# Norm factors spread by TensorE transposes, and gated y stored in two parts: a two-layer decoder trunk on one core

## The chip, the cores and the metric

The kernel runs on one NeuronCore of a Trainium2 chip. The metric is the time of one execution on the device in microseconds; lower is better. All times below are microseconds unless marked otherwise. TensorE is called PE in the profile (its weight loads PEld), VectorE DVE, ScalarE ACT, GpSimd POOL and SyncE, whose queue issues the DMAs, SP.

## The reference

The input is one sequence of 1024 positions with 1024 features. Layer 0 mixes by a gated linear recurrence (LRU), layer 1 by attention with a forget gate (FoX) in 16 heads of 64. Both have a SiLU gate path, and an RMS norm stands before each layer and at the end.

```
def rms_norm(x, g):
    y = xf * lax.rsqrt(jnp.mean(xf * xf, axis=-1, keepdims=True) + EPS)
    return y * g

for i in range(2):
    h = rms_norm(x, norm_g[i])
    x = x + (lru_mixer(h, ...) if i == 0 else fox_mixer(h, ...))
return rms_norm(x, final_g)

# fox_mixer
u = h @ w_in;  q, k, v, gate, f_logit = parts of u
cum = cumsum(log_sigmoid(f_logit + b_f))
logits = q @ k.T * scale + cum[query] - cum[key], causal
o = softmax(logits) @ v
return (o * silu(gate)) @ w_out
```

## The kernel before

Activations lie features by positions: a tile has 128 features on its partitions and 512 positions, a half of the sequence, along the free dimension. To keep float32 accuracy with the faster `float32r` products, each operand is split in a high part (a cast) and a low part (operand minus high part), and each product is three matmuls: high by high, low weight by high, high weight by low. `to_hi` and `to_lo` make the parts; in the profile a cast on ACT is at line 87 and a subtraction at line 98.

The norm needs 1/rms of each position as a row on all partitions. `inv_rms` sums the squares over the features by matmuls with a column of ones (`sscol`), which leaves four columns `rms`, one for each block of 128 positions, with a position on each partition. ACT takes the root and DVE the reciprocal. DVE then multiplies the identity with each column, which gives four diagonal blocks in `rs` (line 153), and one full float32 matmul of a matrix of ones with `rs` sums over the partitions, so that every partition holds the whole row (`rsrow`, line 155). ACT copies it to `rs`. This is done four times, for two halves in each layer.

Layer 1 walks over heads in pairs. For head `hd`, `maxima` makes the scores S of 128 queries against all earlier keys, DVE masks them and takes the maximum, and ACT makes the exponentials p with their sums. `weigh` transposes p on PE (tile `pt`), ACT and DVE split the result in `ph` and `pl`, and PE multiplies both with the values into `O`. Scores and transposed p share two PSUM buffers of two banks each (tag `S`): a new one can be written only when the last reader of the one before the last is through. The sums go through DRAM (`recd`) to come back as a row on 64 partitions (`recb`); POOL multiplies the gate `sg` with it (`scale`, line 765), and after the odd head of a pair the output `yo` with `sg` (`gated`, line 820). For heads 1 to 11 `gated` stores yo to DRAM (`y1d`, line 826), one tile for each of two halves and six pairs.

Beside the attention PE does fill work: the projections of the next pair's keys, queries and gate (`kq_units`, `g_units`, tiles `gps`), and of the next values (`vps`). The gate's projection takes a tanh on ACT into a tile `t` of tag `xp` with two buffers. At heads 12 and 13 the fill is the gate of the last pair and the output projection (`partial`, tile `ops`) of the six stored pairs: `load_y` loads y, `split_loaded` splits it a pair at a time through `beside`, after a named exponential (`seen`) on ACT and a named mask (`masked`) on DVE.

The order on each engine is set by a scheduler at build time from the order of the program text, buffers that come free, and `issue_after`. On the chip each engine then works through its own list in that order.

## Time and profile before

| | |
|---|---|
| median of 3 runs | 1113.87 (1113.86 to 1114.06) |
| the profiled execution's own time | 1113.94 |
| its span, first to last instruction | 1112.2 |
| granted TensorE clock | 1.000 |
| busy: PE, DVE, ACT, POOL | 99%, 68%, 52%, 15% |
| moved by DMA | 105.43 MB |
| 16 products of identity and rms (line 153), DVE | 5.3 |
| 12 casts and 12 subtractions of loaded y, ACT and DVE | 6.8, 9.4 |

The span leaves out what lies before the first and after the last instruction, 1.7 here. Matmuls are pipelined, so their durations overlap: what one costs PE is read from the start of one to the start of the next. In a timeline row a number in brackets is the idle time of that engine just before, with what ended it.

### The profile page before, as it was taken

How to read it: one execution, taken by the hardware profiler on the slowest of the kernel's cores; microseconds unless marked ns; L12 is line 12 of the kernel's file. 1: busy time of each engine (PE TensorE's matmuls, PEld its weight loads, DVE VectorE, ACT ScalarE, POOL GpSimd, SP SyncE). 2: the span in 40 equal slices, each digit the busy share in tenths (PEclk: the TensorE clock that was granted, in tenths of full speed). 3: DMA queues.
4: the chain of work that ended last, by engine and by line, in shares of the span. 5: the costliest groups of instructions: out<-in, count | busy, mean ns of one | idle time of the engine just before them, and what ended most of it. 6: DMA issues, size and time to landing. Idle time of an engine off the chain costs nothing.

```text
span 1112.2 us, 15778 instructions
## 1 busy us (share of the span) xinstructions
PE 1101.9 (99%) x5697; PEld 935.1 (84%) x5697; DVE 755.0 (68%) x1266; ACT 582.4 (52%) x1075; POOL 166.1 (15%) x120
## 2 busy tenths in 40 slices
PE   9999999999999999999999999999999999999997
PEld 7787888888888888988888988889888898878886
DVE  8888755876669687756676566765667655576645
ACT  8487445355453665544555355544555544454435
POOL 1222212111111201421110100101002020010110
PEclk9999999999999999999999999999999999999999
DMA  6111111111112113443334224242142431655444
GB/s 239 48 57 43 51 54 43 48 53 42 62 35 75 48 54 129 129 112 118 101 90 103 91 69 109 72 113 96 53 122 75 103 108 38 185 159 185 142 147 189
DMA packets 63558, 105.43 MB, mean 95 GB/s; under 512 B 9364, under 2 KB 24340, under 8 KB 63480
## 3 DMA queue, kind: packets, MB, share of 16 engines
q1 hardware_dynamic: 63480, 104.42, 31.1%
q8 instruction: 45, 0.74, 0.3%
q14 instruction: 33, 0.27, 0.1%
HBM read 63.30 MB, written 15.93 MB: 71 GB/s over the span
## 4 chain that ended last, share of the span: by engine, by line
PE 93%; issue 3%; DVE 1%; ACT 1%; POOL 1%; DMA 1%; SPq 0%; DVEq 0%; POOLq 0%; ACTq 0%
PE gps L57 33%; PE ops L57 17%; PE ups L57 10%; PE vps L57 8%; PE S L57 6%; PE O L57 6%; PE pt L61 6%; PE turn L57 3%; PE gate L57 2%; POOL wl L98 1%; PE sscol L57 0%; DMA x<-in_xt 0%; DVE hl L232 0%; PE rsrow L57 0%; DMA wf<-in_w 0%
## 5 line engine op out<-in xcount | busy, mean ns | idle before, releaser
L57 PE MATMUL gps<-hh,wh 128*128 128x512 f32 x576 | 228.2, 396 | 0.0
L57 PE MATMUL gps<-hh,wl 128*128 128x512 f32 x576 | 225.6, 392 | 0.2 <-POOL wl L98 0.2
L57 PE MATMUL gps<-hl,wh 128*128 128x512 f32 x576 | 225.5, 392 | 0.0
L87 ACT CAST wh<-wf 128x512 fp32r<-128x512 f32 (+2 forms) x156 | 94.0, 607 | 141.8 <-PE gps L57 56.0
L736 ACT ACTIVATE p<-S,m 128x128 f32<-128x128 f32 (+7 forms) x128 | 94.9, 741 | 140.0 <-DVE m L731 139.1
L98 POOL TENSOR_TENSOR wl<-wf,wh 128x512 fp32r<-128x512 f32 (+1 forms) x60 | 95.6, 1600 | 382.2 <-ACT wh L87 321.7
L98 DVE TENSOR_TENSOR pl<-pt,ph 128x512 fp32r<-128x512 f32 (+1 forms) x198 | 98.7, 540 | 77.0 <-ACT ph L87 76.3
L57 PEld LDWEIGHTS gps<-hl,wh 128*128 128x128 f32 x576 | 108.2, 188 | 23.8
L57 PEld LDWEIGHTS gps<-hh,wl 128*128 128x128 f32 x576 | 108.5, 188 | 19.2 <-POOL wl L98 0.6
L57 PEld LDWEIGHTS gps<-hh,wh 128*128 128x128 f32 x576 | 108.5, 188 | 19.0
L731 DVE CUSTOM_DVE_ANT_0 S<-S,mask 128x128 f32<-128x128 f32 (+7 forms) x128 | 97.3, 760 | 34.2 <-PE S L57 29.6
L765 POOL TENSOR_TENSOR sg<-sg,recb 64x512 f32<-64x512 f32 x32 | 42.8, 1356 | 441.9 <-DMA recb<-recd 407.3
L87 ACT CAST ph<-pt 128x512 fp32r<-128x512 f32 (+1 forms) x198 | 83.5, 472 | 29.1 <-PE pt L61 23.9
L57 PE MATMUL S<-T,U 96*128 96x512 f32 (+7 forms) x384 | 91.7, 347 | 0.0
L98 DVE TENSOR_TENSOR wl<-wf,wh 128x512 fp32r<-128x512 f32 x96 | 68.3, 719 | 24.6 <-ACT wh L87 23.8
L375 DVE TENSOR_TENSOR x<-x,ops 128x512 f32<-128x512 f32 x80 | 54.1, 681 | 40.3 <-PE ops L57 40.3
L57 PEld LDWEIGHTS S<-T,U 128*128 128x128 f32 (+1 forms) x384 | 68.7, 189 | 12.5 <-ACT p L736 0.2
L61 PE MATMUL pt<-ident,p 128*128 128x128 f32 x576 | 79.2, 273 | 0.0
L61 PEld LDWEIGHTS pt<-ident,p 128*128 128x128 f32 x576 | 67.5, 140 | 11.5 <-issue 2.1
L57 PE MATMUL ups<-hh,wh 128*128 128x512 f32 x192 | 75.4, 394 | 1.0 <-ACT hh L89 0.4
L57 PE MATMUL ups<-hh,wl 128*128 128x512 f32 x192 | 75.0, 391 | 0.6 <-POOL wl L98 0.6
L57 PE MATMUL ups<-hl,wh 128*128 128x512 f32 x192 | 75.2, 391 | 0.2 <-DVE hl L232 0.2
(163 smaller groups left out, 2245.4 us busy)
## 6 DMA issues: line engine op xcount, KB each, us to landing
wf<-in_w SPq DMA_DIRECT2D x100, 256.0 KB
wf<-in_wo SPq DMA_DIRECT2D x64, 128.0 KB
U<-qkh SPq DMA_DIRECT2D x64, 128.0 KB
T<-qkh SPq DMA_DIRECT2D x28, 256.0 KB
x1d<-x SPq DMA_DIRECT2D x16, 256.0 KB
wf<-in_wv SPq DMA_DIRECT2D x16, 256.0 KB
U<-qkl SPq DMA_DIRECT2D x32, 128.0 KB
xp<-x1d SPq DMA_DIRECT2D x16, 256.0 KB
```

Source lines behind the costliest of these rows:

```text
L57: pe[0] = nc.tensor.matmul(*args, **kw)
L61: pe[0] = nc.tensor.transpose(*args)
L87: nc.scalar.copy(hi, src)
L98: return eng.tensor_tensor(lo, src, f32(hi), ALU.subtract)
L375: nc.vector.tensor_tensor(x, x, pt, ALU.add)
L731: masked[0] = nc.vector.tensor_tensor_reduce(S[:, :n], S[:, :n], mask[:, SEQ - n :], -1.0, -NEG, ALU.add, ALU.min, accum_out=m)
L736: seen[0] = nc.scalar.activation(p, S[:, :n], AF.Exp, bias=m, scale=-1.0, accum_out=sums[:, i : i + 1])
L765: nc.gpsimd.tensor_tensor(sg, sg, recs[hd // 2][rows, part], ALU.mult)
```

## The change

It has two parts. In `inv_rms` the four products with the identity and the float32 matmul go. Instead PE transposes, for each block of 128 positions, a matrix all of whose 128 columns are the same column of `rms`: the column is read with a step of zero. Each partition of the result holds the row.

In `gated`, for heads 1 to 11, yo is split at once: a cast on ACT to `yh`, a tile of tag `xp`, after the exponential last recorded, and a subtraction on DVE in place, after the mask last recorded. Both parts are stored. `load_y` loads both, and the splits at heads 12 and 13 go, with `split_loaded` and `beside`.

```
-        nc.vector.reciprocal(rms, rms)
+        done = nc.vector.reciprocal(rms, rms)
+        row = ps.tile([P, HALF], F32, tag="O", name="rsrow")[:, : nb * P]
         for b in range(nb):
-            done = nc.vector.tensor_scalar(rs[:, b * P : (b + 1) * P], ident, rms[:, b : b + 1], None, ALU.mult)
-        row = ps.tile([P, HALF], F32, tag="O", name="rsrow")[:, : nb * P]
-        inst = matmul(row, onesf, rs, start=True, stop=True)
+            inst = transpose(row[:, b * P : (b + 1) * P], rms[:, b : b + 1].to_broadcast([P, P]), ident)
         nc.scalar.copy(rs, row)
...
-    y1d = dram.tile([2, KT, P, HALF], F32, name="y1d")
+    y1d = dram.tile([2, KT, 2, P, HALF], F32, name="y1d")
...
             elif hd < 13:
-                nc.sync.dma_start(y1d[c, pair], yo)
+                yh = at.tile([P, HALF], F32R, tag="xp", name="yh", bufs=2)
+                with tc.issue_after(seen[0].ins):
+                    to_hi(yh, yo, nc.scalar)
+                with tc.issue_after(masked[0].ins):
+                    to_lo(yo.bitcast(F32R), yo, yh, nc.vector)
+                for part, y in enumerate((f32(yh), yo)):
+                    nc.sync.dma_start(y1d[c, pair, part], y)
...
             for pair in range(6):
-                nc.sync.dma_start(f32(pair_of_y(c, pair)[1]), y1d[c, pair])
+                for part, y in enumerate(pair_of_y(c, pair)):
+                    nc.sync.dma_start(f32(y), y1d[c, pair, part])
...
-                        beside(g_units(7, (1,)), 0, splits[0]),
+                        g_units(7, (1,)),
                         load_y(1),
-                        beside(beside(partial(todo), 0, splits[0]), 2, splits[1]),
+                        partial(todo),
```

The order of the instructions moves at three kinds of place. First, ACT in head 1, from the exponential of 256 score columns on (p, from S and the maximum m; t is the gate's tanh, wh the high part of a weight, ph of transposed p). Before:

```order
L736 ACTIVATE p,sums<-S,m 128x256
L701 ACTIVATE t_4757<-sg_4630 128x512
L87 CAST ph<-pt 128x512 x2
L736 ACTIVATE p,sums<-S,m 128x384
L87 CAST wh<-wf 128x512
L87 CAST ph<-pt 128x512
L87 CAST ph<-pt 128x384
L736 ACTIVATE p,sums<-S,m 128x512
```

And of the changed kernel, the same stretch:

```order
L735 ACTIVATE p,sums<-S,m 128x256
L87 CAST ph<-pt 128x512 x2
L735 ACTIVATE p,sums<-S,m 128x384
L87 CAST yh<-yo 128x512
L700 ACTIVATE t_4757<-sg_4626 128x512
L87 CAST wh<-wf 128x512
L87 CAST ph<-pt 128x512
L87 CAST ph<-pt 128x384
L735 ACTIVATE p,sums<-S,m 128x512
```

The cast of yo stands behind the exponential of 384 columns, and the tanh, which stood ahead of it, now stands behind the cast; heads 5 and 9 have the same order. Second, DVE in the changed kernel at the same place, from the mask of 384 columns on (S to S with its maximum; `ISA m` reads the maximum out; wl and pl are low parts):

```order
L730 ISA S,m<-S,mask 128x384
L730 ISA m 128x1
L98 TENSOR_TENSOR yo<-yo,yh 128x512
L701 SCALAR_TENSOR_TENSOR sg_4626<-t_4757,sg_4626 128x512
L98 TENSOR_TENSOR wl<-wf,wh 128x512
L730 ISA S,m<-S,mask 128x512
L730 ISA m 128x1
L98 TENSOR_TENSOR pl<-pt,ph 128x512
L98 TENSOR_TENSOR pl<-pt,ph 128x384
```

Before, the product of tanh and gate stood ahead of the two pl that precede the mask of 384 columns, and the two pl of 512 and 384 columns stood ahead of the mask of 512; now the subtraction and that product stand between the two masks, and the mask of 512 ahead of the two pl. Third, ACT in head 3. Before, from the exponential of 256 columns on:

```order
L736 ACTIVATE p,sums<-S,m 128x256
L87 CAST wh<-wf 128x512 x2
L701 ACTIVATE t_5397<-sg_5262 128x512
L87 CAST ph<-pt 128x512 x2
L87 CAST wh<-wf 128x512
L736 ACTIVATE p,sums<-S,m 128x384
L87 CAST wh<-wf 128x512
L87 CAST ph<-pt 128x512
L87 CAST ph<-pt 128x384
L736 ACTIVATE p,sums<-S,m 128x512
```

Of the changed kernel:

```order
L735 ACTIVATE p,sums<-S,m 128x256
L87 CAST wh<-wf 128x512 x2
L87 CAST ph<-pt 128x512 x2
L87 CAST yh<-yo 128x512
L700 ACTIVATE t_5405<-sg_5266 128x512
L735 ACTIVATE p,sums<-S,m 128x384
L87 CAST wh<-wf 128x512 x2
L87 CAST ph<-pt 128x512
L87 CAST ph<-pt 128x384
L735 ACTIVATE p,sums<-S,m 128x512
```

Here the cast and the tanh stand directly ahead of the exponential of 384 columns, and the wh that stood there now stands behind it; heads 7 and 11 have the same order. On PE the order in the attention is as before; the first projections of layer 0 are in another order around the norm rows, which come a few matmuls earlier.

More of the change, by code (lines that the diff above doesn't have):

```diff
@@ L862, in load_y @@
             for pair in range(6):
-                nc.sync.dma_start(f32(pair_of_y(c, pair)[1]), y1d[c, pair])
+                for part, y in enumerate(pair_of_y(c, pair)):
+                    nc.sync.dma_start(f32(y), y1d[c, pair, part])
             yield from ()
-        def split_loaded(c):
-            for pair in range(6):
-                yh, yl = y1[c][pair]
-                with tc.issue_after(seen[0].ins):
-                    to_hi(yh, f32(yl), nc.scalar)
-                with tc.issue_after(masked[0].ins):
-                    to_lo(yl, f32(yl), yh, nc.vector)
-                yield
-        def beside(steps, first, more):
-            for i, _ in enumerate(steps):
-                if i >= first:
-                    next(more, None)
-                yield
         def split_out(db):
@@ L1015, in trunk @@
                     todo = [(db, c) for two in pairs for c in range(2) for db in two]
-                    splits = [split_loaded(c) for c in range(2)]
                     fill = chain(
```

## The prediction

> **What bounds the kernel now.** I read the page first, then the list of waits, then the timeline of single stretches.

> ```profile
> span 1112.2 us, 15778 instructions
> PE 1101.9 (99%) x5697; PEld 935.1 (84%) x5697; DVE 755.0 (68%) x1266; ACT 582.4 (52%) x1075; POOL 166.1 (15%) x120
> PE 93%; issue 3%; DVE 1%; ACT 1%; POOL 1%; DMA 1%; SPq 0%; DVEq 0%; POOLq 0%; ACTq 0%
> ...
> POOL sg L765 <- DMA recb<-recd: 407.3, 16, 41.5
> ```

> TensorE (PE) is busy 99% of the span and carries 93% of the chain that ended last. So an instruction taken from PE is worth its time, one taken from ScalarE (ACT) or VectorE (DVE) is worth nothing unless PE waits for it, and every new wait of PE is paid in full. The last line says that GpSimd (POOL) waits for the reciprocal sums that come back from DRAM: its products are late things by design. That is harmless as long as only a store waits for them.

> **The norm rows (part one).** Timeline of PE, start and duration, around one row and around eight ordinary transposes:

> ```profile
> 441.58 0.61 PE L57 MATMUL gps<-hl,wh 128*128 128x512 f32 x2
> 442.04 1.02 PE L57 MATMUL rsrow<-rs,onesf 128*128 128x512 f32 x2
> 442.49 0.80 PE L57 MATMUL ops<-yh,wh 128*128 128x512 f32 x1
> ...
> 443.13 0.40 PE L57 MATMUL ops<-yh,wl 128*128 128x512 f32 x1
> ...
> 549.95 1.03 PE L61 MATMUL pt<-ident,p 128*128 128x128 f32 x8
> 550.74 0.48 PE L57 MATMUL O<-ph,v 128*128 128x512 f32 x1
> ```

> Durations overlap, so I count starts. Two steps of gps take 0.46 (441.58 to 442.04), 0.23 each. From the row's start to 443.13 there are 1.09, of which one ordinary step is 0.23: the row costs PE 0.86. Eight transposes take 550.74 - 549.95 = 0.79, 0.10 each, so four cost 0.40, say 0.43 with a restart. Four rows: 4 x (0.86 - 0.43) = **1.7 less**. No row shows a stationary operand read with step zero. Bounds: 0.10 each like these transposes, or 0.43 like one of the row's two passes, which would make 16 x 0.43 = 6.9 against 3.4, 3.5 more. It is nearest to the transposes, same shape and same moving operand, so I take 0.10. The 16 DVE products with the identity fall away; DVE is no bound there, and I count nothing, with 0.5 either way for PE stalls near the rows that move.

> [...]

> **The splits that go (part two, gain).** Before, loaded y is split at heads 12 and 13, beside the output projection:

> ```profile
> L87 ACT CAST yhh<-yhl x12: 605/613/622, 967.3 to 991.1; 128x512 fp32r<-128x512 f32 x12
> L98 DVE TENSOR_TENSOR yhl<-yhl,yhh x12: 683/686/1773, 967.9 to 992.4; 128x512 fp32r<-128x512 f32 x12
> ...
> 978.63 0.50 PE L57 MATMUL ops<-yhh,wh 128*128 128x512 f32 x1 [0.20 <-ACT yhh L87]
> 978.96 0.40 PE L57 MATMUL ops<-yhh,wl 128*128 128x512 f32 x1
> 980.36 0.50 PE L57 MATMUL ops<-yhl,wh 128*128 128x512 f32 x1 [1.00 <-DVE yhl L98]
> 980.69 0.39 PE L57 MATMUL ops<-yhh,wh 128*128 128x512 f32 x1
> ```

> PE waits twice. From 978.96 to 980.36 there are 1.40 where a step is 0.23, so 1.17 is lost, with the 0.20 before it **1.4**. Nothing of the split is left between load and matmul, so I credit all of it. (980.36 to 980.69 also shows that the first step after a wait takes 0.33: each wait costs 0.1 more.)

> **The splits that come (part two, price).** The 12 pairs move into heads 1 to 11: a cast yh (0.61) on ACT and a subtraction (0.69) on DVE, 7.3 and 8.2 in all. As busy time these are covered by the idle half of ACT. Their waits are not. The cast reads yo, which POOL has just multiplied, and everything behind it on ACT waits along; the gate's tanh t and the exponentials stand there. The new order puts the first cast of each odd head right behind the exponential of 384 columns (heads 1, 5, 9: place A) or ahead of it (heads 3, 7, 11: place B). Place A, head 1, as it runs before:

> ```profile
> 552.64 2.54 POOL L765 TENSOR_TENSOR sg<-sg,recb 64x512 f32<-64x512 f32 x2 [28.33 <-DMA recb<-recd]
> 555.26 1.29 POOL L820 TENSOR_TENSOR yo<-yo,sg 128x512 f32<-128x512 f32 x1
> ...
> 550.87 0.63 ACT L701 ACTIVATE t<-sg 128x512 f32<-128x512 f32 x1 [0.29 <-DVE sg L699]
> 551.41 1.05 ACT L87 CAST ph<-pt 128x512 fp32r<-128x512 f32 x2
> 554.35 0.58 ACT L736 ACTIVATE p<-S,m 128x384 f32<-128x384 f32 x1 [1.89 <-DVE m L731]
> ...
> 555.02 0.62 ACT L87 CAST wh<-wf 128x512 fp32r<-128x512 f32 x1
> ...
> 558.86 0.69 ACT L736 ACTIVATE p<-S,m 128x512 f32<-128x512 f32 x1 [2.05 <-DVE m L731]
> ...
> 555.67 1.42 DVE L98 TENSOR_TENSOR wl<-wf,wh 128x512 fp32r<-128x512 f32 x1 [1.35 <-ACT wh L87]
> 557.02 1.14 DVE L98 TENSOR_TENSOR pl<-pt,ph 128x512 fp32r<-128x512 f32 x2
> 558.08 0.68 DVE L731 CUSTOM_DVE_ANT_0 S<-S,mask 128x512 f32<-128x512 f32 x1
> ...
> 561.74 0.69 DVE L98 TENSOR_TENSOR wl<-wf,wh 128x512 fp32r<-128x512 f32 x1
> ...
> 556.50 0.62 PE L57 MATMUL S<-T,U 128*128 128x512 f32 x2
> ...
> 558.36 0.49 PE L61 MATMUL pt<-ident,p 128*128 128x128 f32 x3
> ```

> POOL is done at 555.26 + 1.29 = 556.55, while ACT is through with its exponential at 554.9. In the new order ACT stands until 556.6: yh 556.6 to 557.2, t from 557.15, the cast wh 557.65 to 558.3 (a step of ACT on 512 columns is 0.53, half of the 1.05 of the two ph at 551.41), the two ph until 559.2. DVE has in its order the subtraction (557.25 to 557.9), the gate's product (to 558.5), wl (to 559.15), and only then the mask of 512 columns (0.68, to 559.85), then the two pl. The exponential of 512 follows, 559.9 to 560.55. PE's three transposes at 558.36 need a score buffer of two: one is freed by that exponential (560.55), the other by the pl (559.85 + 1.14 = 561.0). So they start at 560.6 instead: 2.2 late, with the restart **2.3**.

> For wl I took the 0.69 of 561.74, not the 1.42 of 555.67, since in the new order POOL's product is over by then. [...] With 1.42 place A would cost 0.7 more.

> Place B, head 3:

> ```profile
> 611.51 2.91 POOL L765 TENSOR_TENSOR sg<-sg,recb 64x512 f32<-64x512 f32 x2 [27.67 <-DMA recb<-recd]
> 614.50 1.30 POOL L820 TENSOR_TENSOR yo<-yo,sg 128x512 f32<-128x512 f32 x1
> ...
> 611.05 1.06 ACT L87 CAST ph<-pt 128x512 fp32r<-128x512 f32 x2
> ...
> 614.54 0.58 ACT L736 ACTIVATE p<-S,m 128x384 f32<-128x384 f32 x1
> ...
> 617.26 1.16 DVE L98 TENSOR_TENSOR pl<-pt,ph 128x512 fp32r<-128x512 f32 x2 [0.31 <-ACT ph L87]
> ...
> 616.94 0.62 PE L57 MATMUL S<-T,U 128*128 128x512 f32 x2
> ...
> 619.50 0.49 PE L61 MATMUL pt<-ident,p 128*128 128x128 f32 x3
> ```

> Here POOL ends at 615.8 and ACT has been free since 612.1. Then yh 615.85, t 616.4, the exponential of 384 columns 616.9 to 617.5 (before: 615.1). The scores at 616.94 overwrite what it reads: PE starts them at 617.55, 0.6 late. Two wh and two ph take ACT 4 x 0.5 more, to 619.45; the two pl on DVE end at 620.65. The transposes, due at 619.50 + 0.6, wait until then: 0.55 more. Two waits, 1.15 and 0.2 of restarts: **1.35**.

> The second cast of each odd head finds yo ready within half a microsecond of ACT; I count it as nothing, up to 0.3. Six first casts: 3 x 2.3 + 3 x 1.35 = **11.0 more**. For the bounds: if PE's slack in these places were half a microsecond larger than I read it at each of the nine waits, 6.5; if the second casts cost 0.3 each and wl stays at 1.42, 15.

> **The DMAs.** SP issues 12 stores more in heads 1 to 11, behind the cast and the subtraction; the loads of U queued behind them come a microsecond later, and so does PE. At heads 12 and 13 it issues 24 loads of 256 KB instead of 12, ahead of the loads xp of the residual:

> ```profile
> 965.00:970.00 5.00, 5.00 (x28) 4.24 (x27) 3.99 (x7) 3.82 (x8) 0.00 (x0) 1.00 0.96 323
> ...
> 975.00:980.00 5.00, 4.16 (x17) 2.76 (x16) 4.35 (x9) 2.67 (x6) 0.00 (x0) 1.00 0.40 115
> ...
> 981.57 0.69 DVE L901 TENSOR_TENSOR xp<-xp,ops 128x512 f32<-128x512 f32 x1
> ```

> The last columns are the share of the DMA engines and GB/s: the queue is full at 965 and worked off by 975. 12 x 262 KB = 3.1 MB more at 323 GB/s is 9.7, so the last of these loads and the xp behind them land by about 984. The add at 981.57, which could now run 1.4 earlier, may wait for its xp up to 3 on DVE. Only its followers on DVE are late; I count 0, with up to 3.

> **Sum.** -1.7 - 1.4 + 11.0 = +7.9. The profiled execution took 1113.94 with a span of 1112.2, the median of the runs is 1113.87, so both are the same to 0.01%: 1113.9 + 7.9 = **1121.8**.

> **Rivals.**
> (1) Faster: PE does not feel ACT's wait. For it: before, PE waits nowhere in heads 1 to 11, and ACT is idle half the time. Against it: the starts above; the break-even is 3.1 / 6 = 0.5 of stall at each first cast, which POOL would reach by ending 1.7 earlier at place A, and it waits for a DMA. It gives 1113.9 - 3.1 = 1110.8. Chance 0.06.
> (2) Only places A stall (another half microsecond of slack at both waits of place B): 1113.9 - 3.1 + 6.9 = 1117.7. Chance 0.13.
> (3) The forecast, and the late xp holds DVE so long that PE waits for its masks: 2 to 3 more, 1124.5. Chance 0.13.
> (4) Step zero is slow on the weight load: 5.2 more than I sum, 1127. Chance 0.03.
> (5) Smaller mixtures that end near no change, 1112 to 1116: 0.05.

> **How the numbers follow.** The forecast itself has 0.60; its own range is 1119 to 1124. The range of 8 in 10 takes in rivals 2 and 3: 1116.5 to 1125.5. The runs agree within 0.02%, but less than 0.2% (2.2) I call no change. Faster 0.06, same 0.05, slower 0.89.

> **What would show it.** Right: an idle ACT before the cast yh with POOL's yo as its releaser, some 2 us at places A and 4 at B, six times; PE idle before pt and S in heads 1, 3, 5, 7, 9, 11, released by ACT p or DVE pl, together about 11; no wait for yhh or yhl at 978 to 980; rsrow as 16 transposes 0.1 apart. Wrong: PE still without waits in heads 1 to 11 (the walk misread the slack), POOL's product much earlier, or transposes of rms 0.4 apart.

## The result and the profile after

The changed kernel takes 1126.9 us (median of 4 executions, 1124.62 to 1129.18) against 1113.88 before: a ratio of 1.0117, 95% interval 1.0094 to 1.0140. It is slower, as forecast, but 13.0 us slower instead of 7.9, and 1126.9 lies above the range of 1116.5 to 1125.5.

The page and the list of waits (in total, times, longest) of the changed kernel, profiled in an execution of 1124.62:

```profile
span 1122.8 us, 15823 instructions
PE 1103.6 (98%) x5705; PEld 936.4 (83%) x5705; DVE 743.5 (66%) x1250; ACT 582.4 (52%) x1075; POOL 161.8 (14%) x120
PE 88%; DMA 3%; DVE 3%; ACT 2%; issue 2%; POOL 1%; SPq 1%; DVEq 0%; POOLq 0%; ACTq 0%
...
ACT yh L87 <- POOL yo L819: 16.7, 6, 4.0
...
PEld pt L61 <- ACT p L735: 7.9, 3, 2.8
...
PE vps L57 <- DVE qkl L98: 2.7, 1, 2.7
```

PE does as much as before, and the chain now runs over DMA, DVE and POOL too. ACT stands six times for POOL's yo, up to 4.0 us. Three waits before pt, released by ACT's exponential, and one before vps, released by DVE, are new. The first of the three, head 1 (place A), on POOL, ACT, DVE and PE:

```profile
555.47 1.29 POOL L819 TENSOR_TENSOR yo<-yo,sg 128x512 f32<-128x512 f32 x1
...
556.79 0.62 ACT L87 CAST yh<-yo 128x512 fp32r<-128x512 f32 x1 [1.56 <-POOL yo L819]
...
560.04 0.69 ACT L735 ACTIVATE p<-S,m 128x512 f32<-128x512 f32 x1 [0.73 <-DVE m L730]
...
557.44 0.69 DVE L98 TENSOR_TENSOR yo<-yo,yh 128x512 fp32r<-128x512 f32 x1 [2.92 <-ACT yh L87]
...
558.65 0.69 DVE L98 TENSOR_TENSOR wl<-wf,wh 128x512 fp32r<-128x512 f32 x1
559.25 0.69 DVE L730 CUSTOM_DVE_ANT_0 S<-S,mask 128x512 f32<-128x512 f32 x1
...
560.87 0.55 PE L61 MATMUL pt<-ident,p 128*128 128x128 f32 x3 [2.11 <-ACT p L735]
```

Read from the top: POOL ends at 556.8, the cast starts there, DVE's subtraction, product and wl follow, the mask of 512 columns ends at 559.9, its exponential at 560.7, and PE goes on. Place B, head 3:

```profile
616.77 1.29 POOL L819 TENSOR_TENSOR yo<-yo,sg 128x512 f32<-128x512 f32 x1
...
618.09 0.62 ACT L87 CAST yh<-yo 128x512 fp32r<-128x512 f32 x1 [3.93 <-POOL yo L819]
...
621.73 1.16 DVE L98 TENSOR_TENSOR pl<-pt,ph 128x512 fp32r<-128x512 f32 x2
...
619.86 0.74 PE L57 MATMUL S<-T,U 128*128 128x512 f32 x2 [0.18 <-ACT p L735]
...
622.94 0.55 PE L61 MATMUL pt<-ident,p 128*128 128x128 f32 x3 [0.22 <-DVE pl L98]
```

The norm rows are as written: four transposes, and 0.35 from their start to the next step.

```profile
440.73 0.60 PE L61 MATMUL rsrow<-ident,rms 128*128 128x128 f32 x4
441.08 0.48 PE L57 MATMUL ops<-yh,wh 128*128 128x512 f32 x1
```

Two things were not in the sum. One is a wait at the layer boundary (DVE, then PE; before, PE waited 0.24 there):

```profile
448.95 0.68 DVE L93 CAST qkh<-gps 128x512 fp32r<-128x512 f32 x1
449.56 1.31 DVE L165 TENSOR_TENSOR sq<-sq 128x512 f32<-128x512 f32 x1
450.79 0.69 DVE L605 TENSOR_TENSOR gps<-gps,rs 128x512 f32<-128x512 f32 x1
451.39 0.68 DVE L98 TENSOR_TENSOR qkl<-gps,qkh 128x512 fp32r<-128x512 f32 x1
...
452.21 0.36 PE L57 MATMUL vps<-wh,hh 128*128 128x272 f32 x1 [2.69 <-DVE qkl L98]
```

The first vps needs a PSUM bank that DVE frees only with qkl. The other is PE's clock. Stretches around head 9 (place A), with PE's busy time first and the granted clock third from the end:

```profile
846.00:850.00 4.00, 1.64 (x8) 1.03 (x7) 3.51 (x7) 3.13 (x7) 0.00 (x0) 1.00 0.62 197
850.00:854.00 4.00, 4.00 (x13) 3.34 (x14) 0.69 (x3) 0.59 (x2) 0.00 (x0) 0.57 0.39 103
854.00:858.00 4.00, 4.00 (x26) 3.52 (x26) 2.84 (x5) 2.55 (x5) 0.79 (x1) 1.00 0.20 61
```

Just after the wait of 2.36 that ends at 849.92, PE runs at half speed: 13 steps in 4 us where the next 4 us hold 26. At a clock of 0.57 those 4 us lose 4 x 0.43 = 1.7, so this execution would have taken 1124.62 - 1.7 = 1122.9 at full clock. The four executions and their mean clocks were 1124.62 at 0.997, 1125.74 at 0.996, 1128.07 at 0.994 and 1129.18 at 0.993: 0.004 of 1123 is 4.5, and they differ by 4.6. Counted so, the median holds 1126.9 - 1122.9 = 4.0 of lost clock.

### The profile page after: what moved, and what is told of

Same layout as the page of the kernel before. It is cut to its first block, busy times and chain, and to the rows that moved or that the text cites. A ratio compares the mean times of both kernels' runs of the same rounds, so it can differ in the third digit from the quotient of the medians.

```text
span 1122.8 us, 15823 instructions
## 1 busy us (share of the span) xinstructions
PE 1103.6 (98%) x5705; PEld 936.4 (83%) x5705; DVE 743.5 (66%) x1250; ACT 582.4 (52%) x1075; POOL 161.8 (14%) x120
## 4 chain that ended last, share of the span: by engine, by line
PE 88%; DMA 3%; DVE 3%; ACT 2%; issue 2%; POOL 1%; SPq 1%; DVEq 0%; POOLq 0%; ACTq 0%
PE gps L57 31%; PE ops L57 17%; PE ups L57 11%; PE vps L57 8%; PE S L57 6%; PE O L57 5%; PE pt L61 4%; PE gate L57 3%; PE turn L57 3%; DMA recb<-recd 2%; DMA recd<-rc 1%; POOL sg L764 1%; POOL yo L819 1%; PE sscol L57 0%; ACT p L735 0%
## 5 line engine op out<-in xcount | busy, mean ns | idle before, releaser
L57 PE MATMUL gps<-hh,wh 128*128 128x512 f32 x576 | 228.9, 397 | 0.0
L57 PE MATMUL gps<-hh,wl 128*128 128x512 f32 x576 | 226.2, 393 | 0.1
L57 PE MATMUL gps<-hl,wh 128*128 128x512 f32 x576 | 225.9, 392 | 0.0
L87 ACT CAST wh<-wf 128x512 fp32r<-128x512 f32 (+2 forms) x156 | 93.5, 607 | 136.5 <-PE gps L57 49.2
L98 DVE TENSOR_TENSOR pl<-pt,ph 128x512 fp32r<-128x512 f32 (+1 forms) x198 | 98.8, 541 | 85.8 <-ACT ph L87 85.2
L98 POOL TENSOR_TENSOR wl<-wf,wh 128x512 fp32r<-128x512 f32 (+1 forms) x60 | 95.0, 1590 | 381.1 <-ACT wh L87 318.5
L57 PEld LDWEIGHTS gps<-hl,wh 128*128 128x128 f32 x576 | 108.6, 188 | 23.7
L57 PEld LDWEIGHTS gps<-hh,wl 128*128 128x128 f32 x576 | 108.9, 189 | 19.2 <-POOL wl L98 0.6
L57 PEld LDWEIGHTS gps<-hh,wh 128*128 128x128 f32 x576 | 108.9, 189 | 19.0
L87 ACT CAST ph<-pt 128x512 fp32r<-128x512 f32 (+1 forms) x198 | 83.6, 472 | 32.3 <-PE pt L61 25.8
L57 PE MATMUL S<-T,U 96*128 96x512 f32 (+7 forms) x384 | 92.0, 348 | 0.5 <-ACT p L735 0.4
L61 PE MATMUL pt<-ident,p 128*128 128x128 f32 x576 | 79.5, 273 | 7.3 <-ACT p L735 6.6
L61 PEld LDWEIGHTS pt<-ident,p 128*128 128x128 f32 x576 | 67.1, 140 | 20.4 <-ACT p L735 7.9
L57 PEld LDWEIGHTS S<-T,U 128*128 128x128 f32 (+1 forms) x384 | 68.6, 189 | 13.9 <-ACT p L735 1.8
L98 DVE TENSOR_TENSOR wl<-wf,wh 128x512 fp32r<-128x512 f32 x96 | 64.2, 676 | 20.4 <-ACT wh L87 19.4
L57 PE MATMUL ups<-hh,wh 128*128 128x512 f32 x192 | 75.3, 393 | 0.8 <-ACT hh L89 0.6
L57 PE MATMUL vps<-wh,hh 128*128 128x256 f32 (+1 forms) x256 | 73.1, 286 | 2.7 <-DVE qkl L98 2.7
L57 PE MATMUL ups<-hl,wh 128*128 128x512 f32 x192 | 75.2, 392 | 0.3 <-DVE hl L231 0.2
```

Source lines behind the costliest of these rows:

```text
L57: pe[0] = nc.tensor.matmul(*args, **kw)
L61: pe[0] = nc.tensor.transpose(*args)
L87: nc.scalar.copy(hi, src)
L98: return eng.tensor_tensor(lo, src, f32(hi), ALU.subtract)
```

## The experiments

### Each part by itself

e1 is part one alone, before with only this edit:

```
-            done = nc.vector.tensor_scalar(rs[:, b * P : (b + 1) * P], ident, rms[:, b : b + 1], None, ALU.mult)
-        inst = matmul(row, onesf, rs, start=True, stop=True)
+            inst = transpose(row[:, b * P : (b + 1) * P], rms[:, b : b + 1].to_broadcast([P, P]), ident)
```

> Part one alone: norm rows by transposes, y stored and split as before. Theory: the wait of 2.7 us that the changed kernel shows at the layer boundary (449.13, first vps, released by DVE qkl) comes from this part, because it moves two projections ahead of output steps on PE. Then the four rows give about -1.2, the start of layer 0 about -0.8 (the 0.60 wait for POOL wl at 100 us is gone in the changed kernel's trace), the boundary +2.4: 1114.4, and up to 1116 in executions in which PE's clock drops behind that wait. Rival, as the prediction had it: only the rows change, 1112.2, and no wait at the boundary.

Measured: 1115.65 (1113.91 to 1116.75), ratio 1.0015, interval 1.0006 to 1.0024. The wait before vps is there with the same 2.69, and in the profiled execution the clock dropped behind it:

```profile
447.00:451.00 4.00, 2.54 (x12) 1.77 (x10) 4.00 (x7) 1.93 (x3) 2.01 (x2) 1.00 0.49 170
451.00:458.00 7.00, 5.77 (x25) 5.80 (x26) 6.84 (x12) 3.62 (x6) 3.13 (x3) 0.54 0.57 190
```

So the part that removes 2 us of PE work makes the kernel slower by itself.

e2 is part two alone: the changed kernel with `inv_rms` as before (the three lines above the other way round).

> Part two alone: y split at once in heads 1 to 11 by ACT and DVE, norm rows as before. Theory: -1.5 for the two waits at heads 12 and 13, three waits of about 2.3 at heads 1, 5, 9 and about 0.9 each at heads 3, 7, 11, 9.7 in all: 1122.1 at full clock. Behind each wait of 2.3 the granted clock may drop to 0.5 for some 3.4 us, 1.6 us each: executions between 1122 and 1127, spread over 2 us. Rival (waits alone, no clock): all executions within 0.5 us of 1122.

Measured: 1125.22 (1124.08 to 1128.07), ratio 1.0105, interval 1.0092 to 1.0119. In the profile PE waits 2.17, 2.45 and 2.20 before pt at places A and 0.23 to 0.26 at places B, and the clock drops behind the one of 2.45 alone, at 706 to 709. The executions are 4 us apart, as the theory with the clock had it, though the longest is 1 us past its 1127; the rival wanted 0.5. Of the two parts, this one holds nearly all of the loss.

### Where part one loses

e3 keeps the transposes in the two rows of layer 0 and gives layer 1 its matmul back:

```
+        first = rms is None
...
+        if first:
+            for b in range(nb):
+                inst = transpose(row[:, b * P : (b + 1) * P], rms[:, b : b + 1].to_broadcast([P, P]), ident)
+        else:
...
+            inst = matmul(row, onesf, rs, start=True, stop=True)
```

> Transposes for the two rows of layer 0 alone, rows of layer 1 and y as before. Theory: the gain of part one lies in layer 0 and its loss at the boundary: 1113.9 - 1.3 = 1112.6, boundary as before with a wait of 0.24. Rival: the boundary wait does not hang on the rows of layer 1: 1114.5.

Measured: 1112.47 (1112.06 to 1113.49), ratio 0.9990, interval 0.9981 to 0.9999. The wait before vps is 0.25. So the two rows of layer 1 cost about 3 us (e1 less e3), though they save PE work like the others.

e5 tells the transposes from the order. DVE writes the column out 128 times, and PE transposes that:

```
+            done = nc.vector.tensor_scalar(rs[:, b * P : (b + 1) * P], onesf, rms[:, b : b + 1], None, ALU.mult)
...
+            inst = transpose(row[:, b * P : (b + 1) * P], rs[:, b * P : (b + 1) * P], ident)
```

> Part one alone, with DVE writing four blocks whose columns all are the same column of rms (in place of four diagonal blocks) and PE transposing these; no step of zero. DVE has the same work as before, and at the layer boundary PE keeps the order of before (output steps between the projections). Theory: the 2.85 at 449 of e1 come from that order and not from the transposes, so they go: 1113.8 - 1.2 to 1.7 = 1112.3, all executions within 1 us, no drop of the clock at 451 to 458. Rival (the transposes themselves bring the wait): 1114.0 to 1116, as e1.

Measured: 1112.50 (1112.09 to 1113.33), ratio 0.9990, interval 0.9982 to 0.9999. PE's timeline at the row and at the first vps:

```profile
441.78 0.60 PE L61 MATMUL rsrow<-ident,rs 128*128 128x128 f32 x4
442.13 0.48 PE L57 MATMUL ops<-yh,wh 128*128 128x512 f32 x1
...
450.82 0.36 PE L57 MATMUL vps<-wh,hh 128*128 128x272 f32 x1 [0.24 <-DVE x L485]
```

The row takes 0.35 here and 0.35 with the step of zero: reading one column 128 times cost PE nothing in these runs. And with four products on DVE again the wait is gone. What they change is the order that the scheduler writes for PE. With them it has, as before, one matmul of a projection, three of an output (ops), the other eleven of the projection, three of the next output, and then vps, whose bank the residual's x frees. Without them, in e1 and the changed kernel, all twelve of the projection come first, then the six, and vps waits for the bank that qkl frees. The transposes are innocent; taking the products away moved an output. No run changes that order alone: that it makes the wait is read from what frees the bank in each trace.

### Where part two loses

e4 issues the first split of each odd head eleven steps later:

```
+                def split():
+                    with tc.issue_after(seen[0].ins):
+                        to_hi(yh, yo, nc.scalar)
...
+                waiting.append([11 if c == 0 else 1, split])
...
+                if waiting:
+                    waiting[0][0] -= 1
+                    if not waiting[0][0]:
+                        waiting.pop(0)[1]()
```

> The changed kernel, with the first split of each odd head issued eleven steps later (behind the exponential of 512 columns), where POOL has long written yo; same casts, subtractions, stores and loads. Theory: what costs is ACT standing for POOL, so the waits of heads 1 to 11 go (9.7 at full clock) and with them the clock drops there: 1113.0, in some executions 1114.6 from the boundary wait of 2.7, which stays. Rival: the casts and subtractions themselves load ACT and DVE too much at these heads, 1118 or more; second rival: the moved casts make new waits for yo's buffer or in front of the next pt, 1115 to 1118.

Measured: 1115.02 (1113.35 to 1115.40), ratio 1.0006, interval 0.9998 to 1.0015. ACT in head 1, and the only wait left on PE there:

```profile
560.83 0.69 ACT L735 ACTIVATE p<-S,m 128x512 f32<-128x512 f32 x1 [2.18 <-DVE m L730]
...
561.50 0.61 ACT L87 CAST yh<-yo 128x512 fp32r<-128x512 f32 x1
...
563.23 0.39 PE L57 MATMUL O<-pl,v 128*128 128x256 f32 x1 [0.17 <-DVE pl L98]
```

The cast follows the exponential at once and waits for nobody. The same work on ACT and DVE, put where POOL is through, is about 12 us cheaper than in the changed kernel, so it was the wait and not the work. The 2.69 at the boundary stays, with half clock behind it at 452 to 456 in the profiled execution. The second rival has a small share: the cast now delays the ph behind it, which costs PE 0.3 to 0.45 at each of heads 1, 5 and 9 with the slower step behind the wait.

e11 gives the splits to POOL (on the kernel with e3's edit), so that nobody waits:

```
-                with tc.issue_after(seen[0].ins):
-                    to_hi(yh, yo, nc.scalar)
-                with tc.issue_after(masked[0].ins):
-                    to_lo(yo.bitcast(F32R), yo, yh, nc.vector)
+                to_hi(yh, yo, nc.gpsimd)
+                to_lo(yo.bitcast(F32R), yo, yh, nc.gpsimd)
```

> Transposes in layer 0 alone, and y split at once but by POOL, cast and subtraction behind its own product, so that neither ACT nor DVE waits for POOL or does the work. If only waits on ACT and DVE count: as e6 less its three waits of 0.33 at the late casts, 1111.2. Rival: POOL's 24 more instructions of 1.3 to 1.6 us slow DVE beside them (wl took 1.42 beside POOL's product and 0.69 elsewhere) or keep the buffers of the tanh too long: 1113 or more.

Measured: 1115.36 (1114.92 to 1116.11), ratio 1.0013, interval 1.0004 to 1.0022. The rival was right:

```profile
553.97 1.29 POOL L826 TENSOR_TENSOR yo<-yo,sg 128x512 f32<-128x512 f32 x1
555.35 0.94 POOL L91 TENSOR_SCALAR yh<-yo 128x512 fp32r<-128x512 f32 x1
...
554.24 1.57 DVE L708 SCALAR_TENSOR_TENSOR sg<-t,sg 128x512 f32<-128x512 f32 x1 [1.26 <-ACT t L707]
555.73 1.09 DVE L98 TENSOR_TENSOR wl<-wf,wh 128x512 fp32r<-128x512 f32 x1
...
557.95 0.55 PE L61 MATMUL pt<-ident,p 128*128 128x128 f32 x3 [0.72 <-DVE pl L98]
```

The product sg takes 1.57 beside POOL's yo and wl 1.09 beside its cast (wl took 0.69 in the changed kernel, where POOL was idle by then); PE waits 0.5 to 0.7 at each place A.

### The clock

e8 is the kernel before with ACT copies ahead of one exponential a head:

```
+                for _ in range(EXTRA.get(hd, 0) if i == 2 else 0):
+                    nc.scalar.copy(S[:, :n], S[:, :n])
```

> The kernel before, with ACT copying the scores of 384 columns onto themselves 5, 6, 7, 8, 9, 10, 11, 12, 14 and 16 times ahead of their exponential, in heads 2 to 11 in this order (0.5 each; the copies only delay). PE waits longer from head to head, by estimate from under 1 to over 5 us. Theory: the granted clock drops to 0.5 only behind waits that fill most of a stretch of some 3.4 us: never behind those under 1.2, by chance behind those of 2 to 3, always behind those of 4 and more, 3.4 or 6.8 us long. Rival 1: the clock drops behind any wait, or has nothing to do with the waits' length. Rival 2: no drop at all here, since the drops of the changed kernel hang on its other work: clock 1.000 and no difference between executions above 0.5 us.

Measured: 1136.11 (1135.65 to 1138.29), ratio 1.0208, interval 1.0192 to 1.0223. The waits were not graded: however many copies, PE's longest wait in a head stayed between 1.38 and 1.89, since PE had other work and then waited for a pl. That miss still gives ten gaps under 2, and the profile, of the fastest execution, has a clock of 1.00 behind each. The slowest execution has a mean clock of 0.997 against 0.999, so a wait may have cost clock there; no profile shows it.

e9 and e10 force the wait (e9: 0 to 9 copies in heads 2 to 11; e10: 2 and 3 by turns):

```
+                    for b in range(4):
+                        transpose(probe[:, b * P : (b + 1) * P], onesf, ident)
+                    nc.scalar.copy(junk, probe)
+                    for _ in range(EXTRA[hd]):
+                        nc.scalar.copy(junk, junk)
+                    for b in range(4):
+                        transpose(probe[:, b * P : (b + 1) * P], junk[:, b * P : (b + 1) * P], ident)
```

> The kernel before with one forced wait of PE in each of heads 2 to 11: four transposes, ACT copies the result and then copies its copy 0, 1, ... 9 times (some 0.55 each), and PE must transpose that before it goes on. Idle gaps of PE from about 1 us (head 2) to 6 us (head 11), 35 us in all. [...] Rival: the drops of the changed kernel come of something else at those places (the DMA or the second engines): clock 1.000 throughout.

> The same with 2 and 3 copies by turns, five times each: gaps of about 2.1 and 2.7 us, the sizes of the changed kernel's waits. Theory: some of the ten are followed by 0.50 for 3.4 us, by chance and more of the longer ones, so executions differ by several us (each drop 1.7). Rival (the length alone decides): all gaps of one length behave alike, and executions agree within 0.5 us.

Measured: e9 1181.94 (1179.40 to 1185.32), ratio 1.0617, interval 1.0596 to 1.0638; e10 1166.97 (1166.25 to 1170.23), ratio 1.0479, interval 1.0465 to 1.0493. Three gaps of e9, two neighbouring stretches that share the gap of 3.30, and the stretch around the last gap:

```profile
651.22 0.66 PE L62 MATMUL probe<-ident,junk 128*128 128x128 f32 x4 [2.10 <-ACT junk L1040]
...
685.15 0.66 PE L62 MATMUL probe<-ident,junk 128*128 128x128 f32 x4 [3.30 <-ACT junk L1040]
...
719.76 1.11 PE L62 MATMUL probe<-ident,junk 128*128 128x128 f32 x4 [4.17 <-ACT junk L1040]
...
680.28:683.69 3.41, 1.57 (x12) 1.20 (x10) 2.18 (x4) 2.16 (x4) 0.00 (x0) 1.00 0.00 0
683.69:687.11 3.42, 1.96 (x12) 1.82 (x13) 0.66 (x1) 1.93 (x4) 0.00 (x0) 1.00 0.50 115
...
715.00:725.00 10.00, 5.83 (x25) 4.90 (x24) 3.38 (x6) 6.00 (x11) 1.77 (x1) 0.66 0.16 55
```

And two gaps of equal length in e10: the two stretches that share the first, then the stretch that holds the second and the one behind it:

```profile
564.60 0.66 PE L62 MATMUL probe<-ident,junk 128*128 128x128 f32 x4 [2.88 <-ACT junk L1040]
...
726.48 0.82 PE L62 MATMUL probe<-ident,junk 128*128 128x128 f32 x4 [2.88 <-ACT junk L1040]
...
559.59:563.00 3.41, 2.13 (x14) 1.67 (x12) 2.66 (x6) 2.44 (x6) 0.00 (x0) 1.00 0.38 121
563.00:566.42 3.42, 1.82 (x12) 1.69 (x13) 1.22 (x2) 2.07 (x4) 1.77 (x1) 1.00 0.47 153
...
723.43:726.84 3.41, 0.53 (x5) 0.36 (x4) 2.08 (x4) 2.91 (x5) 1.77 (x1) 1.00 0.44 126
726.84:730.26 3.42, 3.42 (x12) 2.98 (x11) 0.89 (x2) 1.47 (x3) 0.00 (x0) 0.50 0.20 77
```

The kernel is otherwise that of before, so the drops come from the gaps alone. The profile of e9 has six drops, that of e10 seven. Over all profiles of this case, gaps of PE behind which the clock fell to 0.50: none of 12 that lay between 1.3 and 2.05 (ten in e8, two in e9), none of 7 from 2.10 to 2.20 (changed kernel, e2, e9, e10), 4 of 5 from 2.36 to 2.69 (changed kernel twice, e1, e2, e4), 2 of 3 at 2.88, 5 of 6 at 3.30, and 6 of 6 from 4.17 up. The drops last 3.4 us or 6.8, and once 10.2. Equal gaps (2.88 in e10, 3.30 in e9 and e10) fall on either side, so length alone did not decide.

The starts of the drops show what did. Within one profile they lie whole multiples of 3.413 us apart, to 0.002: in e10 597.13, 689.29 and 726.84 are 27 and 11 such steps apart. So the drops of a profile lie on one grid of 3.41 us, and the gaps are cut on that grid, as the last rows above are. PE's idle time in a stretch is its length less PE's busy time, the first number behind the comma. The 2.88 that did no harm is cut in two, 1.28 and 1.60 idle; the other lies whole in one stretch, and the next runs at 0.50. The harmless 3.30 of e9 is cut in 1.84 and 1.46. Over the profiles of all runs, first and last microseconds left out, no stretch contradicts this reading, that the idle time in one stretch counts: the clock stayed at 1.00 behind some 4100 stretches, with at most 1.84 idle, and fell behind 17, with at least 1.90 (the ends of PE's steps are modelled, so the bound is not known more closely). From half clock it came back behind stretches with at most 0.52 idle and stayed low behind those with 0.65 and more, hence the drops of 6.8.

Where the grid lies against the kernel differs from one profiled execution to the next, and this is the chance in it. The same boundary wait of 2.69 is cut in 1.52 and 1.17 in the profile of the changed kernel and does nothing; in e1 2.04 of it falls in one stretch, in e4 all of it, and the clock drops. The seven gaps from 2.10 to 2.20 were all cut as well (at most 1.79 idle in a stretch), so they were lucky, by estimate: every wait of places A, at 2.1 to 2.5, is longer than the 1.90 that was enough in one stretch, though no run shows a wait under 2.36 with clock lost behind it.

### A version that beats both

e6 has the edits of e3 and e4, e7 those of e4 and e5.

> e4 and e3 together: late splits, transposes in layer 0 alone. If the parts add: e3's 1112.5 less the 1.5 of the splits beside the output projection gives 1111.0; no wait over 0.5 in the trace of heads 1 to 13 and no drop of the clock. Rival: the moved splits cost what they save, 1112.5.

> e4 and e5 together: 1112.3 - 1.5 = 1110.8 if they add; 1111.0 if the two rows of layer 1 are worth nothing; 1113 or more if the boundary wait comes back.

Measured: e6 1112.12 (1111.40 to 1113.25), ratio 0.9988, interval 0.9979 to 0.9997; e7 1112.22 (1111.53 to 1113.15), ratio 0.9987, interval 0.9978 to 0.9996. Both are some 1.6 us faster than before and 14.7 faster than the changed kernel. Against e3 and e5 the late splits bring 0.3, not 1.5: PE's two waits beside the output projection are gone, but the late casts take most of that back. At head 1 two steps of O take 0.22 in e5 (559.95 to 560.17) and 0.68 in e7 (560.08 to 560.76), with a wait of 0.18 for DVE's pl among them; heads 5 and 9 lose as much, 1.4 in all. What is left is below the 1 to 2 us by which executions of one of these kernels differ.

## Why the prediction was wrong

| term | predicted | in the trace |
|---|---|---|
| four norm rows | -1.7 | 4 x (0.86 - 0.35) = -2.0 |
| wait at the layer boundary | none | 2.85 lost at the step, 0.40 before: +2.4 |
| start of layer 0, wait for POOL wl | none | the 0.60 is gone: -0.8 |
| splits beside the output projection | -1.4 | no wait left: -1.5 |
| places A | +6.9 | 2.27 + 2.31 + 2.52 = +7.1 |
| places B | +4.05 | 1.11 + 1.03 + 1.15 = +3.3 |
| stores and loads | 0 | no wait of PE at 965 to 1000: 0 |
| clock behind the waits | none | 1.7 profiled, 4.0 at the median |

The losses at a step are its start-to-start time less that of its like; places B are compared over the whole stretch shown below. Without the clock the terms of the trace give 8.5, and the execution at full clock is 1122.9 - 1113.9 = 9.0 slower; the 0.5 between is the net of small steps, most of them at the start of the kernel, and was not taken apart. That 9.0 comes near the forecast 7.9 is in part luck: the +2.4 that was not in the sum stands against -0.8 at the start and places B and rows that came out 1.1 lower.

**Right.** The mechanism of part two, step by step: ACT behind POOL, 1.56 at place A (forecast some 2) and 3.93 at B (4); the transposes of head 1 at 560.87, forecast for 560.6 on a clock that had POOL end 0.2 earlier; wl at 0.69 and not at 1.42. The second casts and the loads cost nothing: the nearest thing to the late xp of rival 3 is this wait of DVE, of which PE saw nothing.

```profile
994.42 0.69 DVE L891 TENSOR_TENSOR xp<-xp,ops 128x512 f32<-128x512 f32 x1 [0.16 <-DMA xp<-x1d]
```

The step of zero cost nothing (0.35 for four transposes, as in e5 without it), so rival 4 is refuted, although its 1127 is nearly the time that came.

**Wrong: the first step.** "Every new wait of PE is paid in full" made the price of a wait its length. The runs put half clock behind it as well: 4.0 of the 13.0 us at the median, and what carries it out of the range. Drops that start on one grid of 3.41 us and equal gaps with unequal ends (2.88 and 3.30) show that where a wait falls counted beside its length: four of five gaps of 2.36 to 2.69 were followed by half clock, and 1.90 idle in a stretch was enough. What sets the clock so, no trace shows. Half clock behind a wait should have been a rival with a chance of its own.

**Wrong: the layer boundary.** The prediction allowed 0.5 either way for the rows that move and counted nothing. It looked at what the row costs PE and not at what a row that is ready earlier does to the order behind it; e1, e3 and e5 tie the 2.4 to this order. Part one was taken for a gain of 1.7 and is a loss of 1.9 at the median (e1), clock included.

**Mis-sized: places B.** 1.35 each was read: two waits of 1.15 together, and 0.2 of restarts. At head 3 the two waits are 0.34 and 0.38, 0.72 together, with 0.17 in the steps behind them. A third wait that was not read adds 0.2: further on, vps stands for DVE's product sg of the gate, which ends at 626.73. PE at both ends of the place, two rows of before and three of the changed kernel:

```profile
616.70 0.40 PE L57 MATMUL O<-pl,v 128*128 128x512 f32 x1
...
623.31 0.28 PE L57 MATMUL vps<-wh,hl 128*128 128x256 f32 x1
...
619.28 0.40 PE L57 MATMUL O<-pl,v 128*128 128x512 f32 x1
...
626.78 0.38 PE L57 MATMUL vps<-wh,hh 128*128 128x256 f32 x1
627.00 0.28 PE L57 MATMUL vps<-wh,hl 128*128 128x256 f32 x1
```

That is 6.61 before and 7.72 after, 1.11 more. ACT and DVE follow POOL as forecast: the two pl end 4.83 after POOL's yo (622.89 less 618.06), the forecast had 4.85. But PE comes to the scores 1.46 after POOL's end (due at 619.52), where the rows of before gave 1.14 (616.94 less 615.80). A walk through the rows of another kernel is good to some 0.3, which is half of such a small wait and a tenth of those at places A.

Of the rivals none came: places B did wait (2), xp was not late (3), and none had a price for a wait beyond its length.

## What to carry to other kernels

On a kernel that PE bounds, ask of every instruction that is put on an in-order engine who wrote its input last and when: ACT stood up to 4.0 for POOL's yo, and the same cast eleven steps later was nearly free (1115.02 in place of 1126.90). A new wait of PE cost its length here; one that put 1.90 us or more of idle time into one stretch of 3.41 was followed by half clock for 3.41 or 6.83 (once 10.24), by estimate mostly 1.7 or 3.4 more, by where it fell, and executions scattered. From the 1.84 that did no harm, the estimate is that a wait over 2 x 1.84 = 3.7 would not have escaped however it was cut; the six gaps from 4.17 up agree. Where a scheduler sets the order, a cheaper step can be a change of order elsewhere: read the order behind it, down to which bank the next matmul takes.
